# Down-projection of a hybrid encoder: one engine makes all sums, in paired tiles

## The chip, the cores and the metric

The kernel runs on one core of a Trainium2 chip, in one launch. A core has five engines that run side by side: TensorE (PE in the rows; PEld is its weight load), VectorE (DVE), ScalarE (ACT), GpSimd (POOL) and SyncE (SP), whose queue issues nearly all transfers between the off-chip memory and the on-chip buffer (SBUF). TensorE leaves its results in PSUM banks of 128 by 512 float32. The metric is the device time of one execution in microseconds, as the median of several.

## The reference

An encoder trunk of two layers over 1,024 tokens of 1,024 features. Only the second half of a layer matters here:

```python
hf = rms_norm(x, ffn_norm[l]) @ w_up[l]
gate, val = hf[..., :D_FF], hf[..., D_FF:]          # D_FF = 2816
gate = depthwise_conv(gate, conv_w[l], conv_b[l])
x = x + (gelu(gate, approximate=False) * val) @ w_down[l]
```

The change touches the last product, `H @ w_down`, with its addition to `x`.

## The kernel before

Everything is float32. To keep float32's precision, an operand is split into a rounded part (`hi`, made by ScalarE) and a rest (`lo = src - hi`, made by VectorE); a product is three matrix products, hi·hi, hi·lo and lo·hi. `split_x` (L1014 to L1022) does this for a piece of 128 by 512 and puts both parts in one 4 KB tile named `bo`: its line 1017 is the ScalarE copy, its line 1018 the VectorE subtraction.

The hidden features H (22 chunks of 128 rows, 1,024 tokens) are written to DRAM by `up`, chunk by chunk (L1146), and `down` (L1166 to L1293) reads them back with the weights W. It uses Strassen's scheme in Winograd's form: seven products instead of eight, on sums and differences of the four quarters of H and W. The work runs in four groups, `g` = 0 to 3. Groups 0, 1 and 2 have two products each (`j` = 0 in the four banks `pa`, `j` = 1 in the banks `pt` and `pb`), group 3 has one. A group has 11 steps, one for each pair of chunks `k` and `k + 11`; a step of groups 0 to 2 issues 24 matrix products of 128 by 512 columns (line 1289), one of group 3 issues 12. The last two steps of a group are taken output chunk by output chunk, so that banks come free one after the other.

`prep(g, k)` (L1184 to L1220) brings a step's operands: loads by SP, sums and differences through the helper `tt` (line 1175; the engine is its first argument), and four splits. In group 0 it loads `w` and `h` (4 KB tiles, kept for group 1) and a third piece in `r`, and GpSimd makes the two differences. In group 1 it loads both halves of `r` (lines 1201 and 1202), GpSimd makes three sums and VectorE one. In group 2 it loads `dt` and `dh` (lines 1214 and 1215), GpSimd makes two sums in the tile `s` (`ds`), and once `s[:, 0]` has been split, it is loaded again with a piece of W (line 1219) for group 3. Two steps are prepared ahead (`DOWN_AHEAD`).

`evacuate` takes a finished bank. Group 0's eight banks are copied to U and V by ScalarE (line 1233). Group 1's first four are added by VectorE straight to the residual X, each to two places; its second four to U, giving Y, which is added to V; and then 16 sums on GpSimd (`adds`) put U, Y and V on X, two after each `prep` of group 2. Groups 2 and 3 add their banks to X by VectorE. The residual is loaded again in group 1 (`X<-mid`, line 1270).

All tiles come from rings of 4 KB slots: `u` 13, `x` 16, `r` 8, `w` 10, and three half slots. A planner orders each engine's queue at compile time from the order of the code, its own cost estimates and the free slots; at run time each queue, SP's too, is worked off strictly in that order.

Of the kernel before, what the change touches and what calls it, by code (L numbers as in the profile page):

```python
# [9 lines left out]
F32R = mybir.dt.float32r  # L10
# [3 lines left out]
ALU = mybir.AluOpType  # L14
# [13 lines left out]
# the first levels' pairs (s, s ^ x) are taken by elementwise products, the others by matrix products  # L28
# [11 lines left out]
# slots of 4 KB (halves: 2 KB) of the rings  # L40
# [6 lines left out]
# order of the recurrence's steps beside the in-projection, and of the values' tiles  # L47
# [6 lines left out]
# attention: units (kind, head, half of the queries); units whose loads run ahead; for B's four query  # L54
# tiles, the engine that joins the two heads (P: Pool, A: ACT and Pool, D: DVE); key tiles whose low
# part Pool takes; pairs of key tiles that are multiplied whole, in float32
# [6 lines left out]
# out-projection: the mix's chunks, those split ahead, the chunks out  # L63
# [4 lines left out]
# down-projection: steps prepared ahead, steps at a product's end taken feature by feature, the ring  # L68
# that keeps each step's rows, the order that frees them, and when the residual is loaded
# [5 lines left out]
DOWN_FIRST = 3  # L75


def run_beside(main, beside, last):
    """Traces generators side by side: after each step of `main`, as many steps of each in `beside`
    as its ratio asks for. All but `last` are run to their end."""  # L80
# [14 lines left out]
class Trunk:  # L95
    def __init__(self, ctx, tc, ins, out):
# [35 lines left out]
        # what the scores are scaled by, on the queries: A's columns [q q q q], [q q k k], and B's  # L132
        # [q q k k] x 2 heads, where the bias's slope is taken out
# [54 lines left out]
    def rsqrt(self, out, ss, n, shape):  # L188
        """out = (ss / n + eps) ** -0.5"""
        nc = self.nc  # L190
        nc.vector.tensor_scalar(out, ss, 1.0 / n, EPS, op0=ALU.mult, op1=ALU.add)
        w = 1
        for s in shape:
            w *= s
        e = self.mhalf[:, :w]
        nc.gpsimd.tensor_tensor(out, out, e, op=ALU.pow)

    def lower_bounds(self):
        """lbp[:, l, pair] = lower bound, lbp[:, l, 2 + pair] = 1 - lower bound."""
# [23 lines left out]
    def norm(self, X, goff):  # L223
        """X: 8 chunks [128 features, 1024 tokens]. Gives (hi, lo) of x * gain, the token factors
        r [128, 8] token-major and rbc [128, 1024] along the free axis."""
# [37 lines left out]
    def mm_feature_major(self, ps, wh, wl, xh, xl, ks):  # L263
        """ps[128 out, 1024] += W^T X over the chunks; wh/wl(k): stationary, xh/xl[k]: moving."""
# [7 lines left out]
    def mm_token_major(self, ps, t, W, xh, xl, cols):  # L272
        """ps[128 tokens, cols] = X^T W for token tile t; W: pieces of the chunks in order."""
# [40 lines left out]
    def prefetch(self, n, raw=1):  # L314
        """Has the next n pieces split, and `raw` more loaded."""
# [39 lines left out]
    def lam(self, l):  # L355
        """-lambda on every partition, and the sub-norm's gains times 1 - lambda_init"""
# [15 lines left out]
    def proj_cvg(self, p, xh, xl, r):  # L372
        """Values [128, 8, 128] and gates g * sigmoid(g) * gain of head pair p, token-major."""
# [3 lines left out]
        if p == 0:  # L377
            # by chunks of the features first, as they come in, a token tile in each bank; the token
            # factors come later still
# [38 lines left out]
    def proj_cz(self, l, p, xh, xl, rbc):  # L418
        """silu(q) and both directions' forget gates of head pair p, [2 x 64 features, 1024 tokens]."""
# [21 lines left out]
    def proj_a(self, xh, xl, r):  # L441
        """Normed and rotated heads [q x 4], [q q k k], token-major, four token tiles a slot."""
# [1021 lines left out]
```

## Time and profile before

| | |
|---|---|
| runs | 2944.66, 2944.9, 2945.6 us (median 2944.9) |
| the profiled execution | span 2946.1 us; no other time of it is given |
| VectorE, GpSimd, ScalarE busy | 2308.6, 1523.3, 1360.8 us |
| TensorE, as modelled | 2800.5 us |
| `down` of layer 0 | 1222.8 to 1479.5 us of the span |
| `down` of layer 1 | 2683.6 to 2942.2 us of the span |

An engine's busy time is the union of its instructions. A busy TensorE need not be at its peak rate, since the ends of pipelined matrix products are modelled; how far it is from the peak is seen from the time that a known number of them takes. In the rows, "idle before" and the brackets give the time that an engine stood still ahead of an instruction and what released it.

### The profile page before, as it was taken

The page shows a single profiled execution, that of the slowest core. Times are in us where ns is not written, and L with a number is a line of the kernel's source. Part 1 is how long each engine was busy: PE and PEld are TensorE (multiplying, and loading weights), DVE is VectorE, ACT ScalarE, POOL GpSimd, SP SyncE. Part 2 cuts the span into 40 slices and gives each one's busy share as a digit, 9 for nine tenths or more (in the row PEclk, how much of TensorE's full clock was granted, in tenths as well). Part 3 has the DMA queues.
Part 4 walks back from the last instruction along what each step waited for, and adds up shares of the span by engine and source line. Part 5 has one row for each costly group of instructions (what it writes and reads, how often), then busy time and mean ns, then how long its engine had stood idle before and what let it go on. Part 6 is the DMA issues. An engine that isn't in the chain of part 4 may idle for free.

```text
span 2946.1 us, 40451 instructions
## 1 busy us (share of the span) xinstructions
PE 2800.5 (95%) x14984; PEld 2345.0 (80%) x14984; DVE 2308.6 (78%) x3066; ACT 1360.8 (46%) x2443; POOL 1523.3 (52%) x997
## 2 busy tenths in 40 slices
PE   8999999999999999898899999999999999998978
PEld 7999987777778777676799998777777777886757
DVE  5849578896788888889748495888967888887894
ACT  5526467785422222243435363787844222223332
POOL 2517535432366666777324355454324666667681
PEclk9999999999999999999999999999999999999999
DMA  4213262102212222624212043421022222226342
GB/s 145 82 33 102 81 144 69 44 15 70 102 65 86 79 80 79 235 98 160 95 66 83 24 120 104 99 67 44 15 99 74 83 82 72 86 81 237 108 154 75
DMA packets 140228, 267.87 MB, mean 91 GB/s; under 512 B 15104, under 2 KB 72704, under 8 KB 140032
## 3 DMA queue, kind: packets, MB, share of 16 engines
q1 hardware_dynamic: 130240, 235.93, 24.7%
q0 software_dynamic: 9792, 29.36, 3.7%
q8 instruction: 118, 1.93, 0.3%
q14 instruction: 78, 0.64, 0.1%
HBM read 196.03 MB, written 69.21 MB: 90 GB/s over the span
## 4 chain that ended last, share of the span: by engine, by line
PE 46%; DVE 19%; POOL 14%; DMA 9%; issue 7%; ACT 5%; SPq 0%; POOLq 0%; ACTq 0%; DVEq 0%
PE pa L270 10%; PE pa L282 8%; POOL ws L1060 6%; DVE wo L1065 6%; DMA wraw<-w_u 5%; PE pb L861 5%; PE pa L775 5%; DVE bo L1018 4%; PE pt L846 3%; POOL t L1160 3%; PE pa L1289 3%; PE pt L1289 2%; PE pb L1289 2%; ACT wo L1064 2%; PE pt L620 1%
## 5 line engine op out<-in xcount | busy, mean ns | idle before, releaser
L1115 PE MATMUL pt<-bo,wo 128*128 128x512 f32 x1584 | 386.3, 396 | 27.7 <-DVE pu L1122 20.5
L1115 PE MATMUL pb<-bo,wo 128*128 128x512 f32 x1584 | 382.1, 390 | 0.6 <-ACT rbc L1038 0.6
L1115 PEld LDWEIGHTS pt<-bo,wo 128*128 128x128 f32 x1584 | 295.6, 189 | 107.7 <-issue 23.9
L1115 PEld LDWEIGHTS pb<-bo,wo 128*128 128x128 f32 x1584 | 297.2, 188 | 63.2 <-ACT rbc L1038 1.1
L282 PE MATMUL pa<-wh,xh 128*128 128x256 f32 (+1 forms) x864 | 264.7, 307 | 8.0 <-ACT xh L234 8.0
L282 PE MATMUL pa<-wh,xl 128*128 128x256 f32 (+1 forms) x864 | 263.1, 306 | 4.8 <-DVE xl L235 4.8
L775 PE MATMUL pa<-qk,qk 96*128 96x512 f32 (+1 forms) x896 | 257.0, 414 | 10.1 <-DVE nmb L810 3.4
L282 PE MATMUL pa<-wl,xh 128*128 128x256 f32 (+1 forms) x864 | 263.1, 305 | 1.4 <-DVE wl L337 1.4
L1289 PE MATMUL pa<-bo,bo 128*128 128x512 f32 x792 | 209.8, 411 | 48.2 <-DVE bo L1018 21.0
L1289 PEld LDWEIGHTS pa<-bo,bo 128*128 128x128 f32 x792 | 153.8, 198 | 94.2 <-DVE bo L1018 30.6
L1065 DVE TENSOR_TENSOR wo<-ws,wo 128x512 fp32r<-128x512 f32 x176 | 216.1, 1245 | 8.6 <-ACT wo L1064 4.5
L1064 ACT ACTIVATE wo<-ws 128x512 fp32r<-128x512 f32 x176 | 102.0, 624 | 255.4 <-POOL ws L1060 211.7
L856 DVE TENSOR_TENSOR ptl<-pt,pth 128x512 fp32r<-128x512 f32 x240 | 162.1, 684 | 45.5 <-ACT pth L850 44.2
L794 POOL TENSOR_SCALAR pa<-pa,z 128x1024 f32<-128x1024 f32 x96 | 110.4, 1150 | 152.9 <-PE pt L846 104.5
L775 PEld LDWEIGHTS pa<-qk,qk 96*128 96x128 f32 (+1 forms) x896 | 156.8, 190 | 40.6 <-issue 9.6
L810 DVE CUSTOM_DVE_ANT_0 pb<-pa,toep 128x1024 f32<-128x1024 f32 x128 | 153.7, 1218 | 44.6 <-PE pa L775 40.8
L850 ACT ACTIVATE pth<-pt 128x512 fp32r<-128x512 f32 x256 | 149.1, 597 | 76.1 <-PE pt L846 72.1
L282 PEld LDWEIGHTS pa<-wh,xh 128*128 128x128 f32 x864 | 167.2, 194 | 8.1 <-ACT xh L234 8.0
L282 PEld LDWEIGHTS pa<-wh,xl 128*128 128x128 f32 x864 | 166.0, 193 | 5.7 <-DVE xl L235 5.5
L282 PEld LDWEIGHTS pa<-wl,xh 128*128 128x128 f32 x864 | 167.1, 193 | 1.9 <-DVE wl L337 1.6
L1145 DVE TENSOR_TENSOR t<-t,v 128x1024 f32<-128x1024 f32 x44 | 96.6, 2195 | 89.5 <-POOL t L1160 89.5
L1155 POOL TENSOR_TENSOR g<-g,rbc 128x1024 f32<-128x1024 f32 x44 | 109.7, 2492 | 106.8 <-DVE g L1122 106.8
(321 smaller groups left out, 7259.5 us busy)
## 6 DMA issues: line engine op xcount, KB each, us to landing
wraw<-w_u SPq DMA_DIRECT2D x88, 512.0 KB, 4.0
hid<-t SPq DMA_DIRECT2D x44, 512.0 KB, 2.9
dh<-hid SPq DMA_DIRECT2D x44, 512.0 KB, 6.0
bk<-st SPq DMA_DIRECT2D x256, 48.0 KB, 1.7
qk<-bk POOLq DMA_DIRECT2D x32, 384.0 KB, 5.7
dw<-w_d SPq DMA_DIRECT2D x22, 512.0 KB, 6.9
dr<-hid SPq DMA_DIRECT2D x44, 256.0 KB, 5.8
X<-xT SPq DMA_DIRECT2D x16, 512.0 KB, 5.5
```

What stands on the lines that cost most here:

```text
L270: nc.tensor.matmul(ps[:, hf * 512 : hf * 512 + 512], w, x[:, hf * 512 : hf * 512 + 512], start=first, stop=last)
L282: self.nc.tensor.matmul(ps, x[:, ts], w[:, k % kp, :cols], start=first, stop=last)
L775: nc.tensor.matmul(ps[:, hs], q[:rows, o + t * P : o + (t + 1) * P], kk[w][:rows, hs], start=w == 0, stop=w == 1)
L810: nc.vector.tensor_tensor_reduce(e, ps, self.toep[:, o : o + T], scale=-slope, scalar=3.0e38, op0=ALU.add, op1=ALU.min, accum_out=nm)
L850: nc.scalar.activation(hi[:, kk], ps, AF.Copy)
L856: nc.vector.tensor_tensor(lo[:, kk], ps, hi[:, kk], op=ALU.subtract)
L861: nc.tensor.matmul(acc, s, x, start=k == 0 and j == 0, stop=k == NT - 1 and j == len(ops) - 1)
L1060: eng.tensor_tensor(out, a, b, op=op)
L1064: nc.scalar.activation(o[:, 0], src, AF.Copy)
L1065: nc.vector.tensor_tensor(o[:, 1], src, o[:, 0], op=ALU.subtract)
L1115: nc.tensor.matmul(ps, st, mv, start=k + u + v == 0, stop=k == 3 and u == 1)
L1289: nc.tensor.matmul(acc[j][c], a[:, u, c * P : (c + 1) * P], b[:, v], start=q + u + v == 0, stop=q == n - 1 and u == 1)
```

## The change

In `down`, every sum and difference now goes to VectorE; no instruction of `down` is left on GpSimd. Operands are laid out so that two pieces of 128 by 512 lie side by side and one VectorE instruction of 128 by 1,024 makes both sums (`tt(r, p, q)`, `tt(s, p, y)`, `tt(s, z, s)`). The second product's two operands are split together (`split2`: one ScalarE copy and one subtraction, both 128 by 1,024, in two tiles `bw`). For that, the loads are cut into pieces of 256 KB: five in a step of group 0 (three before, of 512, 512 and 256 KB), three in group 1 (two before; `H[k][:, h0]` is loaded a second time), four in group 2 with the reload of `s` (three before). The loads made ahead for the first three steps (`first`) are gone. Group 3's splits take slots of the `x` ring.

Both products of group 1 leave PSUM as copies by ScalarE (tiles E and F), as those of group 0 did. What they give to the residual is summed later by VectorE, in `late_adds`: 24 instructions, eight of 128 by 1,024 and 16 of 128 by 512, three at each of group 2's first eight steps. Of the file's other lines the diff takes away comments only.

```diff
--- before.py
+++ after.py
@@ constants @@
 DOWN_X = 5
-DOWN_FIRST = 3
...
@@ -1160,114 +1159,132 @@
         nc.gpsimd.tensor_tensor(t, t, rbc, op=ALU.mult)
         return t
 
     def down(self, l, H, spill, out):
         nc = self.nc
         W, n = self.i["w_d"][l], NFF // 2
         h0, h1 = slice(0, 512), slice(512, 1024)
-        X, kept, S, U, V, Y, adds = [], {}, {}, [], [], [], []
+        X, kept, S, U, V, E, F, adds = [], {}, {}, [], [], [], [], []
         orders = [list(range(n)), DOWN_ORDER, DOWN_ORDER[::-1], DOWN_ORDER[::-1]]
 
-        def tt(eng, out, a, b, op=ALU.subtract):
-            eng.tensor_tensor(out, a, b, op=op)
-
-        def split(src, slot=self.xslot):
-            return self.split_x(src, None, slot)
-
-        def third(k, slot):
-            r = slot([P, 2, 512], name="dr")
-            nc.sync.dma_start(r[:, 1], H[k + n][:, h1])
-            return r
-
-        first = [third(k, self.xslot) for k in range(DOWN_FIRST)]
+        def tt(out, a, b, op=ALU.subtract):
+            nc.vector.tensor_tensor(out, a, b, op=op)
+        def split(src):
+            o = self.split_x(src, None, self.xslot)
+            return o[:, 0], o[:, 1]
+        def split2(src):
+            hi, lo = (self.xslot([P, 2, 512], F32R, name="bw") for _ in range(2))
+            nc.scalar.activation(hi, src, AF.Copy)
+            tt(lo, src, hi)
+            return (hi[:, 0], lo[:, 0]), (hi[:, 1], lo[:, 1])
+        def load(dst, src):
+            nc.sync.dma_start(dst, src)
 
         def prep(g, k):
             if g == 0:
-                r = first.pop(0) if first else third(k, self.slot)
                 slot = {"r": self.rslot, "w": self.wslot, "u": self.slot}[DOWN_RINGS[k]]
-                w, h = kept[k] = slot([P, T], name="dw"), slot([P, T], name="dh")
-                nc.sync.dma_start(w, W[k])
-                nc.sync.dma_start(h, H[k])
-                one = split(w[:, h0]), split(h[:, h0])
-                tt(nc.gpsimd, r[:, 0], w[:, h0], w[:, h1])
-                tt(nc.gpsimd, r[:, 1], r[:, 1], h[:, h1])
-                return [one, (split(r[:, 0]), split(r[:, 1]))]
+                p, q = kept[k] = slot([P, 2, 512], name="dp"), slot([P, 2, 512], name="dq")
+                b = self.half([P, 512], "dt")
+                load(p[:, 0], W[k][:, h0])
+                load(b, H[k][:, h0])
+                load(q[:, 0], W[k][:, h1])
+                load(q[:, 1], H[k][:, h1])
+                load(p[:, 1], H[k + n][:, h1])
+                one = split(p[:, 0]), split(b)
+                r = self.slot([P, 2, 512], name="dr")
+                tt(r, p, q)
+                return [one, split2(r)]
             if g == 1:
-                w, h = kept.pop(k)
-                r = self.xslot([P, 2, 512], name="dr")
-                nc.sync.dma_start(r[:, 0], W[k + n][:, h1])
-                nc.sync.dma_start(r[:, 1], H[k + n][:, h1])
+                p, q = kept.pop(k)
+                y = self.xslot([P, 2, 512], name="dy")
+                load(p[:, 1], H[k][:, h0])
+                load(y[:, 0], W[k + n][:, h1])
+                load(y[:, 1], H[k + n][:, h1])
                 s = S[k] = (self.slot if len(S) < 9 else self.wslot)([P, 2, 512], name="ds")
-                t = self.half([P, 512], "dt")
-                tt(nc.gpsimd, r[:, 0], r[:, 0], w[:, h1], ALU.add)
-                tt(nc.gpsimd, t, h[:, h1], h[:, h0])
-                one = split(r[:, 0]), split(t)
-                tt(nc.gpsimd, s[:, 0], r[:, 0], w[:, h0])
-                tt(nc.vector, s[:, 1], r[:, 1], t)
-                return [one, (split(s[:, 0]), split(s[:, 1]))]
+                tt(p[:, 1], q[:, 1], p[:, 1])
+                tt(y[:, 0], y[:, 0], q[:, 0], ALU.add)
+                one = split(y[:, 0]), split(p[:, 1])
+                tt(s, p, y)
+                return [one, split2(s)]
             s = S[k]
             if g == 2:
-                w, h = self.half([P, 512], "dt"), self.wslot([P, T], name="dh")
-                nc.sync.dma_start(w, W[k + n][:, h0])
-                nc.sync.dma_start(h, H[k + n])
-                tt(nc.gpsimd, s[:, 0], w, s[:, 0])
-                tt(nc.gpsimd, s[:, 1], h[:, h0], s[:, 1])
-                one = split(s[:, 0]), split(h[:, h1])
-                nc.sync.dma_start(s[:, 0], W[k + n][:, h1])
-                return [one, (split(w), split(h[:, h0]))]
-            return [None, (split(s[:, 0], self.slot), split(s[:, 1], self.wslot))]
+                z, b = self.xslot([P, 2, 512], name="dz"), self.half([P, 512], "dt")
+                load(z[:, 0], W[k + n][:, h0])
+                load(z[:, 1], H[k + n][:, h0])
+                load(b, H[k + n][:, h1])
+                tt(s, z, s, ALU.add)
+                one = split(s[:, 0]), split(b)
+                load(s[:, 0], W[k + n][:, h1])
+                return [one, split2(z)]
+            return [None, split2(s)]
+        def late_adds():
+            for c2 in range(2):
+                u, v, e, f = U[c2], V[c2], E[c2], F[c2]
+                yield f, u, f
+                for j in range(2):
+                    x = X[2 * c2 + j][:, h0]
+                    yield x, x, u[:, j]
+                yield v, v, f
+                yield f, f, e
+                yield e, e, v
+                for j in range(2):
+                    x, y = X[2 * c2 + j], X[4 + 2 * c2 + j]
+                    yield x[:, h1], x[:, h1], f[:, j]
+                    yield y[:, h0], y[:, h0], v[:, j]
+                    yield y[:, h1], y[:, h1], e[:, j]
 
         def evacuate(g, j, c, ps):
-            def pair(ts):
-                return ts[c // 2][:, c % 2]
-
-            def new(ts, slot):
+            if g < 2:
+                ts = ((U, V), (E, F))[g][j]
                 if c % 2 == 0:
-                    ts.append(slot([P, 2, 512], name="du"))
-
-            if g == 0:
-                new((U, V)[j], self.slot)
-                nc.scalar.activation(pair((U, V)[j]), ps, AF.Copy)
+                    ts.append((self.slot, self.wslot)[g]([P, 2, 512], name="du"))
+                nc.scalar.activation(ts[c // 2][:, c % 2], ps, AF.Copy)
                 return
             x, y = X[c], X[4 + c]
-            if (g, j) == (1, 0):
-                tt(nc.vector, x[:, h1], x[:, h1], ps, ALU.add)
-                tt(nc.vector, y[:, h1], y[:, h1], ps, ALU.add)
-            elif (g, j) == (1, 1):
-                new(Y, self.wslot)
-                tt(nc.vector, pair(Y), pair(U), ps, ALU.add)
-                tt(nc.vector, pair(V), pair(V), pair(Y), ALU.add)
-                for z, v in ((x[:, h0], pair(U)), (x[:, h1], pair(Y)), (y[:, h0], pair(V)), (y[:, h1], pair(V))):
-                    adds.append((z, v))
-            elif (g, j) == (2, 0):
-                tt(nc.vector, x[:, h1], x[:, h1], ps, ALU.add)
+            if (g, j) == (2, 0):
+                tt(x[:, h1], x[:, h1], ps, ALU.add)
             elif (g, j) == (2, 1):
-                tt(nc.vector, x[:, h0], x[:, h0], ps, ALU.add)
+                tt(x[:, h0], x[:, h0], ps, ALU.add)
                 if out is not None:
-                    nc.sync.dma_start(out[c], x)
-                    nc.sync.dma_start(out[4 + c][:, h1], y[:, h1])
+                    load(out[c], x)
+                    load(out[4 + c][:, h1], y[:, h1])
             else:
-                tt(nc.vector, y[:, h0], y[:, h0], ps, ALU.add)
+                tt(y[:, h0], y[:, h0], ps, ALU.add)
                 if out is not None:
-                    nc.sync.dma_start(out[4 + c][:, h0], y[:, h0])
+                    load(out[4 + c][:, h0], y[:, h0])
 
         steps = [(g, k) for g in range(4) for k in orders[g]]
-        ready, late = [], []
+        ready, late, adds = [], [], iter(())
         for i, (g, k) in enumerate(steps):
             m = i % n
             while len(ready) < min(len(steps), i + 1 + DOWN_AHEAD):
                 ready.append(prep(*steps[len(ready)]))
-                for _ in range(2):
-                    if adds:
-                        z, v = adds.pop(0)
-                        tt(nc.gpsimd, z, z, v, ALU.add)
+            if g == 2:
+                if m == 0:
+                    adds = late_adds()
+                for _ in range(3):
+                    op = next(adds, None)
+                    if op:
+                        tt(*op, ALU.add)
             if g == 1 and len(X) < KC and m >= DOWN_X:
                 for c in (len(X), len(X) + 1):
                     x = self.rslot([P, T], name="X")
-                    nc.sync.dma_start(x, spill[c])
+                    load(x, spill[c])
                     X.append(x)
             if m == 0:
                 acc = [None, None]
@@ -1286,13 +1303,13 @@
                     for q, ops in late:
                         a, b = ops[j]
                         for u, v in ((0, 0), (0, 1), (1, 0)):
-                            nc.tensor.matmul(acc[j][c], a[:, u, c * P : (c + 1) * P], b[:, v], start=q + u + v == 0, stop=q == n - 1 and u == 1)
+                            nc.tensor.matmul(acc[j][c], a[u][:, c * P : (c + 1) * P], b[v], start=q + u + v == 0, stop=q == n - 1 and u == 1)
                     if m == n - 1:
                         evacuate(g, j, c, acc[j][c])
             late = []
         return X
```

## Rows read from the trace of the kernel before

**Rows 1.** Windows of `down`'s groups: length, busy time of engines, clock, DMA share, GB/s.
```profile
1222.80:1296.80 74.00, 65.10 (x266) 49.63 (x265) 67.10 (x60) 31.15 (x57) 57.36 (x33) 0.98 0.47 171
1296.80:1371.10 74.30, 63.92 (x266) 50.17 (x265) 60.88 (x59) 26.39 (x46) 50.24 (x34) 0.98 0.42 140
1371.10:1449.50 78.40, 66.06 (x266) 52.31 (x265) 71.50 (x81) 35.24 (x62) 49.64 (x28) 0.91 0.34 121
1449.50:1479.50 30.00, 30.00 (x135) 24.86 (x134) 14.30 (x13) 12.15 (x13) 3.43 (x2) 1.00 0.41 133
2683.60:2758.20 74.60, 64.48 (x266) 49.79 (x266) 63.41 (x61) 31.13 (x57) 57.77 (x32) 0.95 0.46 168
2758.20:2832.50 74.30, 63.91 (x265) 50.05 (x264) 61.00 (x58) 26.48 (x46) 51.17 (x34) 0.98 0.42 141
2832.50:2912.10 79.60, 65.92 (x265) 52.21 (x265) 69.68 (x76) 30.61 (x56) 48.74 (x28) 0.91 0.39 132
```

**Rows 2.** The chain that ended last, in group 0 of layer 0: start, length, what.
```profile
1275.17 2.72 PE pa L1289 x12
```

**Rows 3.** TensorE's waits, 1210 to 1480: who waited for whom, total us, times, longest.
```profile
PE pa L1289 <- DVE bo L1018: 10.8, 10, 2.0
PE pa L1289 <- ACT bo L1017: 7.5, 3, 7.0
PE pa L1289 <- DVE X L1175: 5.8, 2, 3.6
```

**Rows 4.** Timeline of group 2, layer 0: start, length, engine, line, operation, tiles.
```profile
1390.36 3.43 POOL L1175 TENSOR_TENSOR X<-X,du 128x512 f32<-128x512 f32 x2
...
1390.87 1.77 DVE L1018 TENSOR_TENSOR bo<-dh,bo 128x512 fp32r<-128x512 f32 x1
...
1392.57 1.77 DVE L1018 TENSOR_TENSOR bo<-dt,bo 128x512 fp32r<-128x512 f32 x1
```

**Rows 5.** Timeline of VectorE late in group 2, layer 0.
```profile
1427.77 1.28 DVE L1018 TENSOR_TENSOR bo<-ds,bo 128x512 fp32r<-128x512 f32 x2
```

**Rows 6.** Line 1175 by engine and tiles: ns minimum/median/maximum, first and last start.
```profile
L1175 POOL TENSOR_TENSOR X<-X,du x32: 1282/1726/1748, 1291.2 to 2861.7; 128x512 f32<-128x512 f32 x32
L1175 DVE TENSOR_TENSOR X<-X,pa x24: 673/675/689, 1365.3 to 2910.7; 128x512 f32<-128x512 f32 x24
```

**Rows 7.** Timeline of group 0, layer 1; in brackets the idle time before and its releaser.
```profile
2699.69 0.64 ACT L1017 ACTIVATE bo<-dr 128x512 fp32r<-128x512 f32 x1 [10.44 <-POOL dr L1175]
...
2712.27 1.22 PE L1289 MATMUL pt<-bo,bo 128*128 128x512 f32 x2 [5.81 <-ACT bo L1017]
```

**Rows 8.** Timeline of SP's queue in group 1, layer 0.
```profile
1317.64 0.37 SPq L1201 DMA_DIRECT2D dr<-w_d  x1
...
1324.44 0.32 SPq L1270 DMA_DIRECT2D X<-mid  x1
1324.86 0.37 SPq L1201 DMA_DIRECT2D dr<-w_d  x1
```

**Rows 9.** Timeline of GpSimd in group 1, layer 0.
```profile
1321.42 1.29 POOL L1175 TENSOR_TENSOR dr<-dr,dw 128x512 f32<-128x512 f32 x1 [1.32 <-DMA dr<-w_d]
```

**Rows 10.** Timeline of group 3, layer 0: a 1,024-wide split of the next layer's weights.
```profile
1461.81 1.06 ACT L336 ACTIVATE wh<-wraw 128x1024 fp32r<-128x1024 f32 x1 [1.87 <-DMA wraw<-w_cvg]
1462.90 1.23 DVE L337 TENSOR_TENSOR wl<-wraw,wh 128x1024 fp32r<-128x1024 f32 x1 [0.31 <-ACT wh L336]
```

**Rows 11.** Line 1233, by tiles, as in rows 6.
```profile
L1233 ACT ACTIVATE du<-pa x8: 577/590/621, 1290.5 to 2757.2; 128x512 f32<-128x512 f32 x8
```

**Rows 12.** SP's waits, 1200 to 1480, as in rows 3.
```profile
SPq L1219 <- DVE bo L1018: 41.2, 11, 12.3
```

**Rows 13.** VectorE's waits in groups 1 and 2 of layer 0 (1296.8 to 1449.5).
```profile
DVE ds L1175 <- DMA dr<-hid: 11.6, 4, 5.1
DVE bo L1018 <- ACT bo L1017: 7.1, 10, 1.9
```

**Rows 14.** Transfers, 1200 to 1300, in 40 slices: GB/s.
```profile
GB/s 185 234 7 34 354 413 419 399 381 419 388 418 419 418 392 397 381 229 0 234 185 252 66 29 180 0 0 0 0 0 0 103 113 65 145 154 56 0 161 301
```

## The prediction, made before the kernel ran

> **What bounds the kernel now.** I read the windows first, cut at the first matrix product of each group of `down`; their columns after the length are TensorE, weight loads, VectorE, ScalarE, GpSimd. Groups 0, 1 and 2 last 74.0, 74.3 and 78.4 us in layer 0, and 74.6, 74.3 and 79.6 in layer 1 [rows 1]. What they would last if TensorE never waited comes from the chain, where 12 matrix products in a row take 2.72 us [rows 2]: a group of 264 is 22 × 2.72 = 59.8 us. So the excess is 14.2, 14.5 and 18.6 in layer 0 and 14.8, 14.5 and 19.8 in layer 1, 96.4 us in all. Group 3 (11 × 2.72 = 29.9) takes 30.0 and has none. 96.4 us is all that a change of `down` can win inside these groups.
>
> TensorE's waits say for what: splits by VectorE (10.8 us), a split by ScalarE (7.5) and sums by VectorE out of the banks (5.8) in layer 0 [rows 3]. The rest of the excess is short gaps and half clock after waits (granted clock 0.91 in group 2).
>
> Then, why VectorE is late. In group 2 its splits of 128 by 512 take 1.77 us and start 1.70 apart, each beside a GpSimd sum [rows 4]; later, with GpSimd still, two take 1.28, so 0.60 a piece and 0.68 for the last [rows 5]. The sums that read a bank never stretch: 673 to 689 ns [rows 6]. So a VectorE operation with two SBUF inputs and a GpSimd sum don't overlap: the pair costs 1.70, of which 0.60 is VectorE's and 1.10 GpSimd's share. GpSimd's own sum goes from 1.28 to 1.73 [rows 6].
>
> Counted for groups 1 and 2 of one layer from the code: GpSimd 33 + 22 + 16 = 71 sums, VectorE 55 + 44 + 4 = 103 operations with two SBUF inputs and 20 out of banks. 71 × 1.10 + 103 × 0.60 + 20 × 0.675 = 78.1 + 61.8 + 13.5 = 153.4 us, against 152.7 measured (74.3 + 78.4) and 119.7 for TensorE. The two engines taken together, not either alone, set the pace of these groups; the closeness is partly luck, since VectorE had idle time as well.
>
> Group 0 is bound otherwise: by the end of `up`, and by GpSimd's queue. In layer 1 ScalarE sat 10.44 us waiting for GpSimd's `dr`, and a split behind another one kept TensorE for 5.81 [rows 7].
>
> Last the loads. In group 1 two `dr` loads go out at 1317.64 and 1324.86, 7.22 apart; the second stands in SP's queue right behind a load of X (1324.44) that waits for a kept tile to come free [rows 8]. From issue to GpSimd's use it is 3.78 us (1317.64 to 1321.42) [rows 9]. This chain is not GpSimd's alone.
>
> **The change, part by part.** *Sums to VectorE.* Durations: 0.60 for 512 columns; for 1,024 the split of a weight takes 1.23, and its ScalarE half 1.06 [rows 10]. A step on VectorE:
> - group 0: two splits, one pair sum, one pair split: 2 × 0.60 + 2 × 1.23 = 3.66;
> - group 1: two sums, two splits, a pair sum, a pair split: 4 × 0.60 + 2 × 1.23 = 4.86;
> - group 2: as group 0, 3.66;
> - group 3: one pair split, 1.23 against TensorE's 2.72.
>
> TensorE's step is 5.44, so each fits. ScalarE has 2 × 0.62 + 1.06 = 2.3 a step and is no limit (0.62 from [rows 7], where one takes 0.64).
>
> *Residual later.* Group 1's eight banks leave as ScalarE copies of 0.59 [rows 11], against 16 VectorE sums of 0.675 and four more. The copies hide behind the 1.36 us (half of 2.72) between finished banks, so the 5.8 us of waits on X at the seams go. Uncovered, eight would cost 4.7. The 24 late sums are 8 × 1.23 + 16 × 0.60 = 19.4 us. They fall on eight steps: 8 × 3.66 + 19.4 = 48.7 against 8 × 5.44 = 43.5, 5.2 us too much unless VectorE runs ahead. Behind them in VectorE's queue stand the next splits, and for those TensorE waits.
>
> Groups 1 and 2 together: 11 × 4.86 + 11 × 3.66 + 19.4 + 8 × 0.675 = 118.6 us on VectorE, beside 119.7 on TensorE. Before it was 153.4. That is a near tie, with no room.
>
> The Trainium skill says of a saturated VectorE that moving some work to ScalarE "(or even GPSIMD) may make sense", and in the same place that the two share a port, so that it might not help ("Perfetto Trace Analysis", Optimizing Scalar/DVE Operations). By the first half the 16 single late sums belong on GpSimd, and VectorE would have 109.0 us. By [rows 4] each costs 1.10 there instead of 0.60, so 126.6 in place of 118.6; the trace bears out the second half.
>
> *Loads.* Group 0's bytes stay, in five issues instead of three; group 1 gets 256 KB more per step, group 2 about as many in one more issue. At the start transfers run at about 400 GB/s [rows 14] and are ahead of need; a group 1 step's 0.79 MB in 5.44 us is 145 GB/s, where 140 is moved now [rows 1]. I cost this at nothing, covered by matrix products; were it exposed, one load's 3.78 us at each of three starts and two layers is 23 us. The X loads still stand ahead of later loads and still wait for kept tiles, which now come free after VectorE's sums. I keep the chain's period of 7.22 for three steps of group 1: 3 × (7.22 − 5.44) = 5.3 us.
>
> *The start.* GpSimd's wait in group 0 is gone, and `first` with it; the end of `up` still has GpSimd work and still needs VectorE for its banks. Bounds: all 14 us stay, or none. The nearest row is the 5.81 [rows 7], which goes, so I keep 8.
>
> *Clock.* A wait that stays still costs clock: group 1 has 0.98 now, 1.5 us of 74. I leave 1.5 a layer.
>
> Sum of excess left per layer: 8 (group 0) + 5.3 (group 1) + 5.2 (group 2) + 1.5 = 20.0, twice 40.0. Gain 96.4 − 40.0 = 56.4. The profiled execution's span is 2946.1 and no other time of it is given; 2946.1 − 56.4 = 2889.7. The runs' median stands 1.2 below that span: 2888.5, so 2889.
>
> **The rivals.**
>
> *VectorE becomes the bound.* In groups 1 and 2 it waited 18.7 us of 152.7 for transfers and ScalarE [rows 13], and stood idle 20.3 in all (152.7 − 60.9 − 71.5). If 14% idle stays, 118.6 needs 137.9, an excess of 18.2 where I have 10.5: 7.7 more a layer, 2904. With the full 7.22 period on 19 steps (11 and 8), the excess is 8 + 1.5 + 19 × 1.78 = 43.3 a layer and the time 2935. For it: the near tie. Against: X loads are few, and 19 steps in one chain need every load behind the one before. 2904 to 2935, chance 0.20.
>
> *A serial chain, slower than before.* Place: SP's in-order queue in groups 1 and 2, where a step's loads stand behind one that waits for VectorE's split of the step before; today the reload of `s` waits 41.2 us that way [rows 12]. Price: the pair split lengthens the chain by (1.06 + 1.23) − (0.62 + 0.68) = 0.99, so 7.22 becomes 8.21. On 19 steps that is 9.5 + 19 × 2.77 = 62.1 a layer, 124.3 in all, 27.9 more than now: 2973. It decides from a period of 7.65: 9.5 + 19 × 2.21 = 51.5 a layer, in both layers 6.6 us more than today's 96.4. For it: the same shape of code, longer instructions. Against: the pair sum comes ahead of the pair split in the code, and the next load needs only the sum and the single splits. Chance of slower 0.13, of a period between (within 0.2%) 0.05.
>
> By the Trainium skill, where VectorE isn't saturated but causes bubbles on another engine, "breaking up instructions may allow work to be completed sooner" (the same page and section). The pairs do the opposite; no row of before shows a pair in `down`.
>
> *Nearly everything is won.* If VectorE runs ahead during groups 0 and 1 (22 steps with 1.78 and 0.58 to spare each), only the start stays: 96.4 − 16 = 80.4, so 2864. Chance 0.12.
>
> **Chances and range.** The forecast, 2868 to 2904 as its own range, has 0.50; nearly all 0.12; VectorE's bound 0.20; no change 0.05; slower 0.13. Faster is 0.50 + 0.12 + 0.20 = 0.82. 0.2% (6 us) is what a measurement of this kernel can tell from no change. The range runs from 2862, under the full win, to 2938, just past VectorE's bound; what lies outside is mainly the slower case.
>
> **What the profile would show.** Right: no GpSimd instruction of `down`; every VectorE operation of 512 columns near 0.68 and every pair near 1.23 to 1.29 in groups 1 to 3; no wait of TensorE on X at the seam of groups 1 and 2; groups 1 and 2 at 65 to 67 us each, group 0 near 68, group 3 at 30. The step on group 2 is wrong if VectorE is busy through its first eight steps and TensorE still waits over 6 us there. The prediction is wrong if loads go out one by one, 7 us or more apart, through groups 1 and 2; if GpSimd's end of `up` holds the first steps longer than now; or if group 3 exceeds 30, because its splits now share the `x` ring with the next layer's norm.

## The result and the profile after

The changed kernel takes 2922.8 us (2921.9 to 2927.7), the kernel before 2945.3 (2944.7 to 2948.6) beside it: 0.9919 of its time [0.9904, 0.9934], so 22 us were won where 56 had been forecast. The profiled executions, with spans of 2946.1 and 2921.4 us, differ by 24.7.

The windows of the kernel after, cut at the same matrix products as [rows 1], with the last 84 products of `up` ahead of each layer's groups 0 to 2 (length, then TensorE, weight loads, VectorE, ScalarE, GpSimd, clock, DMA share, GB/s):

```profile
1202.10:1227.00 24.90, 20.95 (x86) 16.85 (x85) 16.06 (x19) 3.84 (x6) 9.78 (x5) 0.93 0.82 288
1227.00:1295.30 68.30, 62.03 (x265) 50.38 (x264) 58.78 (x69) 30.75 (x45) 15.84 (x3) 0.95 0.60 209
1295.30:1355.10 59.80, 59.80 (x265) 49.54 (x264) 47.82 (x57) 28.89 (x41) 0.00 (x0) 1.00 0.49 165
1355.10:1438.50 83.40, 70.80 (x266) 52.78 (x266) 57.28 (x70) 30.07 (x41) 0.00 (x0) 0.92 0.42 135
...
2652.30:2675.20 22.90, 19.30 (x85) 15.68 (x84) 15.99 (x19) 3.85 (x6) 8.55 (x5) 1.00 0.80 282
2675.20:2745.10 69.90, 62.76 (x265) 50.96 (x264) 59.54 (x69) 30.74 (x45) 16.77 (x3) 0.95 0.60 213
2745.10:2805.00 59.90, 59.90 (x266) 49.60 (x265) 48.60 (x57) 28.65 (x41) 0.00 (x0) 1.00 0.46 158
2805.00:2887.40 82.40, 68.54 (x265) 51.82 (x264) 54.58 (x63) 25.83 (x36) 0.00 (x0) 0.94 0.38 125
```

The same 84 products in the kernel before:

```profile
1201.70:1222.80 21.10, 19.31 (x85) 15.69 (x84) 17.11 (x16) 5.13 (x8) 14.51 (x9) 1.00 0.76 286
2662.40:2683.60 21.20, 19.31 (x85) 15.68 (x84) 17.05 (x16) 5.09 (x8) 14.42 (x9) 1.00 0.76 284
```

Read against [rows 1], the two layers together: group 0 gains 10.4 us and group 1 gains 28.9, all that it had to give (59.8 is TensorE's time without a wait, granted clock 1.00). Group 2 loses 7.8, though it was to gain most, and `up`'s end loses 5.5 (24.9 and 22.9 for 21.1 and 21.2). Group 3 stays at 30. That is 10.4 + 28.9 − 7.8 − 5.5 = 26.0 us, beside 24.7 in the span; 1.3 us were lost outside these windows.

In the rows from here on, lines 1016 and 1017 are the copy and the subtraction of `split_x`, 1174 is `tt`, 1183 the copy in `split2`, 1188 `load` and 1306 the matrix products of `down`; 1114 and 1121 are products and bank sums of `up`.

TensorE's waits, 1210 to 1470, answer to [rows 3] (who waited for whom, total us, times, longest):

```profile
PE pa L1306 <- ACT bo L1016: 10.3, 7, 2.9
PE pt L1306 <- DVE bw L1174: 5.9, 1, 5.9
PE pt L1114 <- DVE pu L1121: 3.9, 1, 3.9
```

The waits for X are gone. The third row is `up`'s end, the second the start of group 0, and the first lies in group 2: a ScalarE copy is late there seven times, where before it was late once, by 7.0 us. Behind it stands VectorE, and behind VectorE the loads. VectorE's waits in that group (1355.1 to 1438.5):

```profile
DVE ds L1174 <- DMA dz<-hid: 20.4, 6, 4.4
```

The waits of SP's queue in the same window are all for VectorE, this one above all:

```profile
SPq L1188 <- DVE bo L1017: 47.7, 15, 7.1
```

None is for TensorE, which frees the slots of the `x` ring. By these rows the loads wait for their turn in the queue, not for a slot.

Then the timelines of one stretch of group 2, first SP's queue (start, length, engine, line, transfer), then VectorE, with the idle time before and its releaser in brackets:

```profile
1399.25 0.33 SPq L1188 DMA_DIRECT2D ds<-w_d  x1
1399.85 0.32 SPq L1188 DMA_DIRECT2D dt<-hid  x1
1400.26 0.38 SPq L1188 DMA_DIRECT2D dz<-w_d  x1
1400.70 0.42 SPq L1188 DMA_DIRECT2D dz<-hid  x1
1408.28 0.33 SPq L1188 DMA_DIRECT2D ds<-w_d  x1
```

```profile
1396.55 1.22 DVE L1174 TENSOR_TENSOR ds<-dz,ds 128x1024 f32<-128x1024 f32 x1 [4.16 <-DMA dz<-hid]
1398.53 0.69 DVE L1017 TENSOR_TENSOR bo<-ds,bo 128x512 fp32r<-128x512 f32 x1 [0.76 <-ACT bo L1016]
1399.14 0.68 DVE L1017 TENSOR_TENSOR bo<-dt,bo 128x512 fp32r<-128x512 f32 x1
...
1405.58 1.23 DVE L1174 TENSOR_TENSOR ds<-dz,ds 128x1024 f32<-128x1024 f32 x1 [4.35 <-DMA dz<-hid]
1407.56 0.69 DVE L1017 TENSOR_TENSOR bo<-ds,bo 128x512 fp32r<-128x512 f32 x1 [0.76 <-ACT bo L1016]
```

A closed chain: the sum `ds` is made and split (1396.55 to 1399.22, 2.67 us); only then can the reload of `s[:, 0]` leave, and behind it in SP's queue stand `dt` and both halves of the next `dz` (1.48 us to the issue at 1400.70); its data let the next sum start 4.88 us later, at 1405.58. 2.67 + 1.48 + 4.88 = 9.03 us for this step, where TensorE needs 5.44. The group's eleven sums `ds` start 7.1 to 10.5 us apart, 8.8 on average.

Last the start of group 0 in layer 0, where [rows 7] had its wait for GpSimd:

```profile
1227.77 7.75 DVE L1174 TENSOR_TENSOR dr<-dp,dq 128x1024 f32<-128x1024 f32 x6
1236.64 1.21 DVE L1174 TENSOR_TENSOR bw<-dr,bw 128x1024 fp32r<-128x1024 f32 x1
1237.91 2.08 PE L1306 MATMUL pt<-bw,bw 128*128 128x512 f32 x4 [5.92 <-DVE bw L1174]
```

Six pair differences stand in VectorE's queue ahead of the first pair split that TensorE needs. And at `up`'s end `down`'s first split stands ahead of the sum that frees `up`'s bank:

```profile
1216.96 0.69 DVE L1017 TENSOR_TENSOR bo<-dp,bo 128x512 fp32r<-128x512 f32 x1 [4.46 <-ACT bo L1016]
...
1218.96 0.69 DVE L1121 TENSOR_TENSOR pu<-pu,pt 128x512 f32<-128x512 f32 x1
1219.79 4.58 PE L1114 MATMUL pt<-bo,wo 128*128 128x512 f32 x12 [3.95 <-DVE pu L1121]
```

### The profile page after: what moved, and what is told of

It reads as the page before. It is cut to its first block, busy times and chain, and to the rows that moved or that the text cites. A ratio compares the mean times of both kernels' runs of the same rounds, so it can differ in the third digit from the quotient of the medians.

```text
span 2921.4 us, 40354 instructions
## 1 busy us (share of the span) xinstructions
PE 2797.9 (96%) x14984; PEld 2345.9 (80%) x14984; DVE 2260.8 (77%) x3082; ACT 1359.5 (47%) x2371; POOL 1236.8 (42%) x811
## 4 chain that ended last, share of the span: by engine, by line
PE 27%; DVE 9%; POOL 6%; DMA 5%; issue 3%; ACT 3%; SPq 0%; ACTq 0%; DVEq 0%; POOLq 0%
PE pa L269 5%; PE pa L281 4%; POOL ws L1059 3%; DVE wo L1064 3%; PE pb L860 2%; PE pa L774 2%; DMA wraw<-w_u 2%; PE pt L1306 2%; PE pa L1306 2%; PE pb L1306 2%; DMA dz<-hid 2%; PE pt L845 2%; POOL t L1159 1%; ACT wo L1063 1%; PE pb L619 1%
## 5 line engine op out<-in xcount | busy, mean ns | idle before, releaser
L1064 DVE TENSOR_TENSOR wo<-wraw,wo 128x512 fp32r<-128x512 f32 x132 | 149.7, 1137 | 18.3 <-ACT wo L1063 16.1
L812 ACT ACTIVATE pb<-pb,nmb 128x1024 f32<-128x1024 f32 x128 | 147.1, 1151 | 32.7 <-DVE nmb L809 27.0
```

The lines of the kernel that those rows point to most:

```text
L812: nc.scalar.activation(e, e, AF.Exp, bias=nm, scale=-1.0, accum_out=z[:, t, i : i + 1])
L1064: nc.vector.tensor_tensor(o[:, 1], src, o[:, 0], op=ALU.subtract)
```

## The experiments

All changes are against the kernel after, unless the text says otherwise. Ratios are to the kernel before, run beside them, with their 95% intervals.

### What lengthens group 2: the queue or VectorE

*The reload of `s` and the `dt` load on another queue.*

```diff
-                load(b, H[k + n][:, h1])
+                nc.gpsimd.dma_start(b, H[k + n][:, h1])
...
-                load(s[:, 0], W[k + n][:, h1])
+                nc.gpsimd.dma_start(s[:, 0], W[k + n][:, h1])
```

> The changed kernel, with group 2's reload of s and its load of dt issued from GpSimd's queue, which is empty in down; SP keeps the z loads alone. Theory A (queue order): group 2 lasts 83 us because each z load stands in SP's queue behind a reload and a dt load that wait for VectorE's splits of the step before; then group 2 falls to 62 to 67 us in each layer and the time to 2885 to 2892 us. Theory B (VectorE is overloaded by the 24 late sums, 19.4 us in eight steps): group 2 stays above 78 us and the time above 2912 us.

Measured: 2888.7 us, 0.981 [0.9794, 0.9827]; group 2 takes 70.5 and 63.7 us in the two layers, for 83.4 and 82.4. The time is as the first theory had it; layer 0's group stays above its 67 us. Not an instruction of VectorE was touched, so the queue's order carried at least 13 and 19 of the 23 us in excess. What kept the rest was not tested. In SP's queue `z` still stands behind transfers that wait for VectorE: loads of the next layer's weights in layer 0 (25.5 us of SP's waits in group 2), stores of the result in layer 1 (17.3 us ahead of the last `z`).

*Without the late sums.* The kernel leaves out what groups 0 and 1 give to the residual.

```diff
-                    adds = late_adds()
+                    adds = iter(())
```

> The changed kernel without the late sums: what group 0 and group 1 give to the residual is left out of the output. Theory A (queue order): the z loads still go out one by one, so group 2 stays at 74 to 83 us and the time at 2905 to 2923 us. Theory B (VectorE overloaded): group 2 falls to 60 to 64 us and the time to 2880 to 2888 us.

Measured: 2927.3 us, 0.9934 [0.9915, 0.9953]; group 2 takes 84.8 and 82.0 us, the time and layer 0's group a little above the first theory's ranges. Its window in layer 0 and VectorE's wait there:

```profile
1354.90:1439.70 84.80, 71.04 (x266) 53.41 (x265) 45.30 (x52) 31.69 (x43) 0.00 (x0) 0.90 0.42 137
```

```profile
DVE ds L1174 <- DMA dz<-hid: 30.5, 9, 4.7
```

VectorE has 12.0 us less to do (45.3 for 57.3) and waits 10.1 us longer for the same loads. An overload of VectorE by the late sums is ruled out as what sets the group's length. With them VectorE has no pause from 1350.43 to 1384.13, and the three steps there take 10.36, 10.50 and 8.15 us from one sum `ds` to the next; without them the same steps take 10.51, 8.60 and 8.15 us, with waits for loads in place of the late sums.

*`z` back in the ring of `w`.* In group 2 the kernel before had its whole-width tile in the `w` ring and the other in a half slot. The change put `z` in the `x` ring, where the splits' tiles live (five slots a step with `z`), which come free as TensorE finishes with them.

```diff
-                z, b = self.xslot([P, 2, 512], name="dz"), self.half([P, 512], "dt")
+                z, b = self.wslot([P, 2, 512], name="dz"), self.half([P, 512], "dt")
```

> The changed kernel with group 2's tile z in the w ring instead of the x ring; all loads on SP as in the change. Theory A in its narrow form: z loads stand behind the reloads because the planner gives them a slot of the x ring only when TensorE frees one; in the w ring they go out up to four ahead, group 2 falls to 62 to 68 us and the time to 2886 to 2894 us, as with the other queue. Rival: it is the reloads' and dt's waits themselves that hold the next step, wherever z lies; group 2 stays above 75 us and the time above 2908 us.

Measured: 2875.6 us, 0.976 [0.9742, 0.9778], 10 us under the expectation. Group 2 in both layers:

```profile
1354.60:1414.40 59.80, 59.80 (x265) 49.53 (x264) 58.61 (x73) 32.25 (x42) 0.00 (x0) 1.00 0.54 179
2780.90:2840.70 59.80, 59.80 (x265) 49.53 (x264) 53.66 (x64) 25.96 (x35) 0.00 (x0) 1.00 0.43 146
```

SP's queue there, as above:

```profile
1364.37 0.33 SPq L1188 DMA_DIRECT2D dz<-w_d  x1
1364.75 0.42 SPq L1188 DMA_DIRECT2D dz<-hid  x1
1366.64 0.33 SPq L1188 DMA_DIRECT2D dz<-w_d  x1
1367.02 0.42 SPq L1188 DMA_DIRECT2D dz<-hid  x1
1369.58 0.33 SPq L1188 DMA_DIRECT2D ds<-w_d  x1
1370.18 0.32 SPq L1188 DMA_DIRECT2D dt<-hid  x1
1371.32 0.33 SPq L1188 DMA_DIRECT2D dz<-w_d  x1
```

The reload of `s` is still in SP's queue, behind the same split. But two `dz`, each in its two halves, go out ahead of it, so the loads run further ahead and no chain closes: VectorE waits for no load in this window, where it waited 20.4 us. This one word in the code is worth 47 us (0.9919 − 0.976), more than the whole change gained, and it takes all of group 2's excess away. With the late sums VectorE is busy for 58.61 of 59.80 us and TensorE never waits.

### Was GpSimd the cost that the change took away

*The engine alone.* The kernel before, with all its loads, tiles and single sums; only `tt` issues on VectorE whatever its argument.

```diff
-            eng.tensor_tensor(out, a, b, op=op)
+            nc.vector.tensor_tensor(out, a, b, op=op)
```

> The kernel before with every sum of down on VectorE, nothing else changed: no pairs, the old loads, group 1's banks still added by VectorE. If moving the sums off GpSimd is what gains (sums that no longer block VectorE's splits for 1.10 us each), groups 1 and 2 together fall from 153 us to 122 to 138 us a layer and the time to 2890 to 2925 us. If the gain is from the pairs and from ScalarE emptying group 1's banks, the time stays above 2935 us.

Measured: 2865.0 us, 0.9731 [0.9716, 0.9747], 25 us under the expectation. `up`'s last 84 products and groups 0 to 2 in layer 0:

```profile
1202.40:1227.30 24.90, 20.92 (x85) 16.82 (x84) 20.93 (x28) 8.24 (x14) 7.99 (x4) 0.93 0.80 300
1227.30:1288.00 60.70, 60.16 (x265) 49.40 (x264) 55.74 (x83) 28.22 (x51) 10.58 (x3) 1.00 0.52 194
1288.00:1347.90 59.90, 59.90 (x266) 49.58 (x265) 54.43 (x90) 26.58 (x47) 0.00 (x0) 1.00 0.51 170
1347.90:1409.80 61.90, 60.17 (x266) 49.49 (x265) 61.83 (x107) 34.64 (x61) 0.00 (x0) 1.00 0.41 142
```

One line gains 79 us (0.0269 of 2946.6), so the rest of the change loses some 55 (0.9919 − 0.9731 of the same). VectorE is busy for 61.83 of 61.90 us in group 2, and the group is only 2 us longer than TensorE needs (3.7 us in layer 1).

*The engine and the evacuation.* To this, also against the kernel before, come the ScalarE copies of group 1 and the 24 `late_adds` on VectorE, as the change has them; loads and tiles of `prep` stay as before.

```diff
-            if (g, j) == (1, 0):
-                tt(nc.vector, x[:, h1], x[:, h1], ps, ALU.add)
...
+            if g < 2:
+                ts = ((U, V), (E, F))[g][j]
...
+                    op = next(adds, None)
+                    if op:
+                        tt(nc.vector, *op, ALU.add)
```

> The engine move alone, with the change's other half added: group 1's banks leave by ScalarE and the 24 late sums are made by VectorE in group 2; loads and single sums as before the change. In the engine move alone, group 2 has an excess of 2.0 and 3.5 us a layer over 59.8. If the late sums overload VectorE (19.4 us in eight steps), the excess grows to 5 to 8 us a layer and the time is 2869 to 2876 us; if ScalarE's emptying of the banks is worth more than they cost, the time is 2860 to 2864 us.

Measured: 2864.6 us, 0.9722 [0.9702, 0.9742], not to be told from the engine alone. Group 2 takes 61.9 and 61.7 us. ScalarE's copies and the late sums neither win nor cost once VectorE makes all sums.

*The late sums on GpSimd*, with `z` in the `x` ring (first) and in the `w` ring (second).

```diff
-                        tt(*op, ALU.add)
+                        nc.gpsimd.tensor_tensor(*op, op=ALU.add)
```

> The changed kernel with the 24 late sums on GpSimd. Theory A with blocking: group 2's chain of loads stays and its VectorE links get longer beside GpSimd, so group 2 lasts 85 to 95 us and the time is 2928 to 2945 us. Theory B (VectorE overloaded): VectorE is relieved of 19.4 us, group 2 falls below 76 us and the time below 2910 us.

> z in the w ring, and the 24 late sums on GpSimd. With z in the w ring group 2 has no excess. If GpSimd's sums block VectorE's splits (1.10 us each for 512 columns) also where no chain of loads stands behind it, group 2 rises from 59.8 to 66 to 80 us and the time from 2876 to 2888 to 2916 us. If moving work to GpSimd is free while VectorE has room, the time stays at 2872 to 2880 us.

Measured: 2946.1 us, 1.0004 [0.9989, 1.0019], with group 2 at 95.4 and 92.5 (time and group a little above the expectation); and, as expected, 2906.6 us, 0.9854 [0.9828, 0.9879], with group 2 at 78.3 and 71.1, for 59.8 and 59.8 with the same sums on VectorE. Some 28 us (0.0094 of 2948.9) for 24 instructions. The second kernel's group 2 in layer 0:

```profile
1355.20:1433.50 78.30, 66.80 (x265) 52.08 (x264) 71.39 (x52) 30.36 (x40) 43.52 (x19) 0.93 0.40 129
```

VectorE has 21 instructions fewer than with the same sums on VectorE (52 for 73) and is busy for 71.39 us instead of 58.61: the others have become longer. VectorE and GpSimd stand beside each other in this group thus, VectorE first:

```profile
1357.81 2.90 DVE L1017 TENSOR_TENSOR bo<-ds,bo 128x512 fp32r<-128x512 f32 x1
1360.64 3.42 DVE L1174 TENSOR_TENSOR ds<-dz,ds 128x1024 f32<-128x1024 f32 x1
1363.98 1.78 DVE L1017 TENSOR_TENSOR bo<-dt,bo 128x512 fp32r<-128x512 f32 x1
...
1375.71 2.29 DVE L1174 TENSOR_TENSOR bw<-dz,bw 128x1024 fp32r<-128x1024 f32 x1
```

```profile
1356.76 6.21 POOL L1283 TENSOR_TENSOR du<-du,du 128x1024 f32<-128x1024 f32 x2
1362.93 3.98 POOL L1283 TENSOR_TENSOR X<-X,du 128x512 f32<-128x512 f32 x2
...
1373.51 3.40 POOL L1283 TENSOR_TENSOR X<-X,du 128x512 f32<-128x512 f32 x2
```

None of these VectorE operations is at its own length: the first two stand beside GpSimd sums of 1,024, the last two beside sums of 512.

*Group 0's pair differences on GpSimd*, with `z` in the `w` ring.

```diff
-                tt(r, p, q)
+                nc.gpsimd.tensor_tensor(r, p, q, op=ALU.subtract)
```

> z in the w ring, and group 0's 11 pair differences on GpSimd, so that they stand in no queue with the first splits. If the order in VectorE's queue alone makes the first step long, group 0 falls from 68.4 to 60 to 64 us and the time from 2876 to 2860 to 2870 us. If GpSimd's differences, of about 2.4 us each, block the pair splits or come late behind up's own GpSimd work, group 0 stays at 66 us or more and the time above 2871 us.

Measured: 2904.0 us, 0.9857 [0.9829, 0.9885]; group 0 takes 81.7 and 84.8 us, for 68.4 and 68.5 with VectorE's, as the second half of the expectation had it. VectorE's timeline beside GpSimd's differences, and after a pause of theirs:

```profile
1233.69 3.37 DVE L1174 TENSOR_TENSOR bw<-dr,bw 128x1024 fp32r<-128x1024 f32 x1
1236.99 2.88 DVE L1017 TENSOR_TENSOR bo<-dp,bo 128x512 fp32r<-128x512 f32 x1
...
1257.03 1.21 DVE L1174 TENSOR_TENSOR bw<-dr,bw 128x1024 fp32r<-128x1024 f32 x1
1258.16 0.68 DVE L1017 TENSOR_TENSOR bo<-dp,bo 128x512 fp32r<-128x512 f32 x1
```

### The start

*The differences' tile `dr` in the `x` ring*, which the kernel before used for its first three steps.

```diff
-                r = self.slot([P, 2, 512], name="dr")
+                r = self.xslot([P, 2, 512], name="dr")
```

> The changed kernel with group 0's pair difference r in the x ring instead of the u ring, which has free slots for six of them at the start. Theory S: the first step of group 0 takes 14 us instead of 5.4 because six differences of 1.2 us run ahead of the first pair split in VectorE's queue; in the x ring no more than two or three can, so the first step falls to 5.4 to 8 us, group 0 to 60 to 63 us, and the time to 2904 to 2912 us. Rival: the end of up holds VectorE or the banks at that point; then group 0 stays at 68 us and the time at 2920 us or more.

Measured: 2910.6 us, 0.9886 [0.9862, 0.991], as expected. Group 0 falls to 61.3 and 61.2 us: with fewer tiles to run ahead in, the differences no longer go out six in a row, and a pair split stands after each. But `up`'s last 84 products now take 28.3 and 27.9 us. Of the 7.0 and 8.7 us won in group 0, 3.4 and 5.0 are given back there.

*Both tiles moved.* `z` in `w` and `dr` in `x`, the two edits above.

> Both of the edits of this call, r in the x ring and z in the w ring. If the two causes are apart, their gains add: 2868 to 2880 us. If VectorE's 24 late sums are then the limit, group 2 stays at 66 us or more in both layers and the time above 2880 us.

Measured: 2867.7 us, 0.9733 [0.9715, 0.975], at the lower edge of the expectation; groups 1 and 2 at 59.8 in both layers, group 0 at 61.4 and 62.2, `up`'s end at 28.0 and 26.8. With these two words the changed kernel, pairs and loads included, comes out where the engine alone does (0.9731), not better.

*`down`'s first three steps behind a sum of `up`*: VectorE's operations of these steps stand in its queue behind the sum of the fourth of seven products in `up`'s last chunk. Once on top of the two moved tiles, once on the kernel with the engine and the evacuation.

```diff
             add(u3, u2, p7)
+            self.tail = nc.cur_bb.bb.instructions[-1]
...
-                ready.append(prep(*steps[len(ready)]))
+                if len(ready) < 3:
+                    with self.tc.issue_after(self.tail):
+                        ready.append(prep(*steps[len(ready)]))
+                else:
+                    ready.append(prep(*steps[len(ready)]))
```

> r in the x ring and z in the w ring, and VectorE's operations of the first three steps of down queued behind up's sum of its fourth product (the second into pu's second half) of the last chunk. Theory U: up's last chunk takes 27 to 28 us there instead of 19.6 to 21 because VectorE's queue holds down's first splits and differences, which wait for their loads to land, ahead of up's sums, and TensorE waits for the bank. Then the chunk falls to 20 to 23 us in each layer and the time from 2868 to 2853 to 2861 us. Rival: the work is only moved, and the first step of down waits for its splits as long as up did; the time stays at 2864 to 2872 us.

> The engine move with group 1's banks by ScalarE and late sums, loads as before the change, and the same queueing behind up's sum. Theory U: the last chunk of up falls from 24.6 to 20 to 22 us and the time from 2864.5 to 2855 to 2861 us. Rival: the first step of down waits instead, 2862 to 2868 us.

Measured: 2863.4 us, 0.9713 [0.9682, 0.9743], and 2858.0 us, 0.9699 [0.9671, 0.9728]. `up`'s end falls to 19.0 us in all four places, the time of 84 products without a wait (7 × 2.72), and group 0 rises to 70.4 and 68.2, and to 66.1 and 65.2. In layer 0, end and group 0 together were 28.0 + 61.4 = 89.4 and are 19.0 + 70.4 = 89.4; in the other kernel 24.6 + 60.7 = 85.3, and now 85.1. In layer 1 little was won: 88.9 became 87.2, and 85.3 became 84.2. The wait was for the most part moved, not removed, as the rivals had it. The second kernel's time lies in the first theory's range all the same, but the stages don't bear that theory out: of the 10.8 us between its profiled span and that of the kernel without the edit (2853.3 and 2864.1), 7.7 lie outside `up`'s end and `down`, where the two have the same code. It has the lowest median of all, 3% under the kernel before, but its interval overlaps with those of the kernels without this edit, so only its gain over the two kernels of the study, before and after, is shown.

## Why the prediction was wrong, step by step

**The step that failed is *Loads*:** "I cost this at nothing, covered by matrix products". It counted bytes and issues, and these were indeed no limit (135 GB/s in group 2, where the kernel with `z` in the other ring moves 179). It didn't ask which ring the new tile `z` takes and so where its load can stand in SP's queue. Group 2 kept an excess over 59.8 of 23.6 and 22.6 us, where 5.2 a layer were left for it: 36 us in all, about the 34 by which the forecast missed. The chain's cause is shown by three runs: other queue, 70.5 and 63.7; other ring, 59.8; fewer sums, no change. That the planner places `dz` late because an `x` slot comes free late is read from the code and fits the second run; the planner's own reckoning is not shown. The prediction's own sign of being wrong, loads that go out one by one and 7 us or more apart, came true in group 2 (6.3 to 13.9 us between the `dz` of one step and the next in layer 0, all but one above 7) and not in group 1.

**The serial-chain rival named the place and the mechanism**, a load behind one that waits for VectorE's split of the step before. It had the period at 8.21 us (9.03 measured in the step shown, 8.8 on average), by adding 0.99 to a period of before instead of summing the links. It put the chain into groups 1 and 2. In group 1 there was none, though `y` lies in the `x` ring too, and so the kernel stayed ahead of the one before; that no step there loads again a tile that it has just split is the reason by the code, and was not tested.

**What bounds the kernel now** was right in the mechanism: GpSimd's sums, which hold up VectorE's operations, paced groups 1 and 2. Moved to VectorE, with nothing else changed, group 1 falls to TensorE's time and group 2 to within 2.1 us of it in layer 0; that it is the holding up is seen where the late sums go to GpSimd (VectorE busy for 71.39 us instead of 58.61, with fewer instructions). That the sum of 153.4 us met the 152.7 measured stays luck, as the text half says: VectorE was busy for only 60.88 + 71.50 = 132.4 of them [rows 1].

***Sums to VectorE*:** pairs take 1.21 to 1.23 us and single operations 0.68, as costed. The result lies in the time range of the rival "VectorE becomes the bound" (2904 to 2935; its 14% idle is 13.3 by its own numbers, 20.3 of 152.7, which makes 2902), and that rival is nevertheless false: group 1 won all that it could and group 2 lost, and VectorE waited there for loads.

***Residual later*:** the copies are hidden, and the waits for X at the seams are gone, as said. The 5.2 us for the late sums are 0: with `z` in the other ring TensorE never waits in group 2. VectorE had room to run ahead (busy for 47.82 of group 1's 59.80 us).

***Loads* of X in group 1:** three steps at a period of 7.22 were to cost 5.3 us a layer; they cost none.

***The start*:** 8 was kept for group 0, and 8.5 and 10.1 remained. The size is right for another reason than the one given: not what is left of an old wait, but a new one of 5.9 us for six differences in a row. That it fits is luck. `up`'s end wasn't costed, though the text saw that it needs VectorE: 5.5 us.

***Clock*:** 1.5 us a layer was left for it. The granted clock was 0.95 in group 0 and 0.92 and 0.94 in group 2, and the waits cost more than their length: TensorE's waits in group 2 of layer 0 add up to 12.3 of its 23.6 us of excess. Twelve products that take 2.72 us without a wait took 4.79 us, from their start to the next product's, behind the wait in this row; the granted clock was 0.64 there, so most of that time it stood at the lower of its two levels, 1.2 GHz:

```profile
1390.24 4.95 PE L1306 MATMUL pa<-bo,bo 128*128 128x512 f32 x12 [1.56 <-ACT bo L1016]
```

With `z` in the `w` ring, and no wait, group 2 has 1.00.

**The sum:** 40.0 us of excess were to stay, and 8.5 + 10.1 + 0.1 + 23.6 + 22.6 = 64.9 stayed, with 5.5 new at `up`'s end. 96.4 − 70.4 = 26.0, beside the span's 24.7.

**The Trainium skill's advice** that some work of a saturated VectorE "(or even GPSIMD) may make sense" ("Perfetto Trace Analysis", Optimizing Scalar/DVE Operations) fails here in every form tried: VectorE at 58.61 of 59.80 us leaves TensorE without a wait, and 24 sums given to GpSimd cost 18.5 and 11.3 us of group 2. The Trainium skill's caveat in the same place, that VectorE and GpSimd share a port and moving work between them might not help, is the half that the runs bear out, as far as the time goes; a port is nothing that they show. The Trainium skill's other rule there, "breaking up instructions may allow work to be completed sooner", was weighed against the pairs; the runs show nothing for it, since kernels with single sums and with pairs come out alike (0.9731 and 0.9733). No run changes the pairs alone.

What stays open: some 6 to 11 us in layer 0 between `up`'s end and group 1 in the best versions (85.1 to 89.4 against 19.0 + 59.8 = 78.8). Reordering moved them; whether the loads of the first steps land too late was not separated.

## What to carry to other kernels

When an edit moves a tile to another ring, write out the new order of the loads on the issuing queue and close the loop: from the split that a load waits for, through every load behind it, to the next split. Where the sum of the links exceeded TensorE's step, as in group 2, the pace was that sum, though VectorE was busy for only 57.28 of 83.40 us and the engines that move the data for 0.42 of the time. Where VectorE and GpSimd both make sums at once, try moving the engine alone first, as one line: here it was worth more than the whole change.

## What the runs showed of the hardware

How long a GpSimd sum holds up a VectorE operation goes by GpSimd's width, not VectorE's own: a VectorE split of 128 by 512 takes 0.68 us alone, 1.77 beside a GpSimd sum of 512 [rows 4], and 2.88 to 2.90 beside one of 1,024; a pair of 1,024 takes 1.21 alone, 2.29 beside the narrow sum and 3.37 to 3.42 beside the wide one. The stretch is 1.1 us beside the narrow sum and 2.2 beside the wide one, whatever VectorE's own width. The operations of `up` that carry scalars pay it as well: `t` on line 1156 takes 3.38 us beside the wide differences and 1.28 without. So a GpSimd pair holds VectorE about as long as two single sums would (2.2 us for 2 × 1.1).

A pair gives VectorE nearly nothing over two singles: 1.22 us against 1.28 for two in a row [rows 5].
